# Layer 1's modulations: weighted and added by ScalarE and GpSimd during layer 0's second FFN matrix, with TensorE left to sum over the partitions

## The chip, the cores and the metric

The kernel runs on one core of one Trainium2 chip. The metric is the device time of one execution in microseconds. The core's engines work beside each other, each through its own queue in order: TensorE (PE) multiplies matrices out of SBUF into PSUM, VectorE (DVE), ScalarE (ACT) and GpSimd (POOL) work on tiles, and SyncE (SP) issues most of the DMA transfers. An engine waits for another by semaphores that the framework sets.

## The reference

The model is a trunk of two layers on 256 context tokens and 1024 latent tokens of width 1024. A conditioning vector gives each layer six modulation vectors (shift, scale and gate for the mixer and for the FFN), once for latent and once for context tokens. Cut to that and the places where it is used:

```python
for l in range(DEPTH):
    m_lat = (silu(c) @ w_mod[l] + b_mod[l])        # w_mod[l] is 1024 x 6144
    m_ctx = (silu(c_ctx) @ w_mod[l] + b_mod[l])
    sh1, sc1, ga1, sh2, sc2, ga2 = split(m_lat, 6)  # likewise for the context
    pl = modulate(rms_norm(x, g_mix[l]), sh1, sc1) @ w_in[l]
    ...                                             # four mixers, w_out, gated residual ga1
    x = x + ga2 * (squared_relu(modulate(rms_norm(x, g_ffn[l]), sh2, sc2) @ w_ffn1[l]) @ w_ffn2[l])
```

All data is float32.

## The kernel before

Activations lie with features on the partitions and tokens on the free axis: 256 context columns and two groups of 512 latent columns. Each large product is made of three matmuls on split operands (`mm3`, L141 to L143: high by high, high by low, low by high). The splits are made by ScalarE (the high part, a copy, L130) and by GpSimd (the low part, a subtraction, L246) for weights, and by VectorE (L1420) for the hidden activations.

The modulations of a layer are made in three **banks** of 2048 columns by `mod_bank` (L306). For each of eight slices k of 128 rows of `w_mod` it loads two halves of 128x1024 (L315, on SP's queue) and issues four matmuls of 128x512 (L319). Their stationary operand is `csil`, the two conditioning vectors' slice in 32 columns, so each result fills one of four 32-partition groups of a PSUM tile `po`. After eight slices ScalarE copies `po` to SBUF, four transposes (L328) turn it, and two additions on VectorE (L333) put it, with the bias, into `mods`. `mods` (the function) does this bank by bank and adds the scale vectors `ms` for banks 0 and 2.

Layer 1's three banks are made at three places. Bank 0 is made in layer 0's `ffn`, in the loop over pairs of hidden chunks (L1428): two slices after each of the first four pairs, with the halves in `u` tiles (25 buffers). Bank 1 is a stream of its own in `weave` in layer 1's first stage (L1490), beside the last part of the norm (`pending`) and the first attention projection (`p_attn`); its halves are in `e` tiles (3 buffers). Bank 2 is a third stream beside the second LRU mixer and an attention projection (L1498).

One iteration of the FFN2 loop has two chunks fc. It loads and splits two row blocks of `w_ffn2` (`wrows`: one in `wh`/`wl` tiles, one in `u` tiles), loads two chunks of activations (`e<-m`), has ScalarE copy them to `u` tiles and VectorE subtract (`act`, L1419 and L1420), and then runs 24 accumulations: eight output blocks for each of the three token groups, each of six matmuls into one of seven PSUM buffers (`pm`, `qk`, `pt`), with an evacuation by VectorE (L136) that multiplies by the gate and adds to x.

`weave` and the loops set the order in which the program is written; a list scheduler of the framework then fixes each engine's own order from it before the kernel runs.

Of the kernel before, what the change touches and what calls it, by code (L numbers as in the profile page):

```python
# [10 lines left out]
ALU = mybir.AluOpType  # L11
AX = mybir.AxisListType

P = 128
# [4 lines left out]
KD = D // P  # L19
NT = T // P  # L20
DEPTH = 2
# [7 lines left out]
C_GMIX, C_GFFN, C_BMOD, C_SCW, C_SCB, C_SD, C_SG = 0, 8, 16, 64, 88, 94, 96  # L29
# [64 lines left out]
class Net:  # L94
# [55 lines left out]
    def setup(self):  # L150
        nc = self.nc

        rnd = self.const([P, 4 * P], "rnd", F32R)
        raw = self.B(4 * P)
        nc.sync.dma_start(raw, self.I["cst"][:, 0:4 * P])
        self.copy_a(rnd, raw)
        self.identr, self.wmask = rnd[:, 0:P], rnd[:, P:4 * P]
        self.ident = f(self.identr)
        cst = self.const([P, 2 * P], "cst")
        nc.sync.dma_start(cst, self.I["cst"][:, K_LE:K_LE + 2 * P])  # L160
        self.one = self.const([P, 1], "one")
        nc.vector.memset(self.one, 1.0)
        self.le = cst[:, 0:P]
        self.ge = cst[:, P:2 * P]
        self.mhalf = self.const([P, 1], "mhalf")
        nc.vector.memset(self.mhalf, -0.5)
        cT = self.const([P, KD, 2], "cT")
        nc.sync.dma_start(cT, self.I["cT"])
        th = self.const([P, KD, 2], "cth")
        self.act(th, cT, AF.Tanh, scale=0.5)  # L170
        ch = self.const([P, KD, 2], "cth2")
        nc.vector.tensor_scalar(ch, cT, 0.5, None, op0=ALU.mult)

        self.csil = self.const([P, 2 * KD + 30], "csil")
        nc.vector.memset(self.csil, 0.0)
        self.stt(self.csil[:, 0:2 * KD].rearrange("p (k j) -> p k j", j=2), th, 1.0, ch, ALU.add, ALU.mult)
        self.L = [self.layer_params(l) for l in range(DEPTH)]

    def late_setup(self):
# [126 lines left out]
    def mod_bank(self, l, b, land, tag="po"):  # L306

        nc = self.nc
        ps = self.PS(tag)
        for k in range(KD):  # L310
            raws = []
            for hf in range(2):
                raw = f(land())[:, :1024]
# [4 lines left out]
            for cg in range(4):  # L318
# [2 lines left out]
                                 start=k == 0, stop=k == KD - 1, skip_group_check=True,  # L321
                                 tile_position=(0, 32 * cg))
            yield 1.8
        sb = self.B()
        self.copy_a(sb, ps)
        pt = self.PS(tag)
# [6 lines left out]
            nc.vector.tensor_add(m[:, 16 * b:16 * b + 16, st].rearrange("p (c q) -> p c q", c=4), v[:, :, :, st], bm)  # L333

    def mods(self, l, banks, land, tag="po"):
        nc = self.nc
        p = self.L[l]
        if "mods" not in p:
            p["mods"] = self.const([P, 48, 2], f"mods{l}")
            p["s"] = [self.const([P, 8, 2], f"ms{l}{i}") for i in range(2)]  # L340
        for b in banks:
            yield from self.mod_bank(l, b, land, tag)
            if b != 1:
                i, j, cg = (0, 1, C_GMIX) if b == 0 else (1, 4, C_GFFN)
                for st in range(2):
                    self.stt(p["s"][i][:, :, st], p["mods"][:, 8 * j:8 * j + 8, st], 1.0, p["pp"][:, cg:cg + 8],
                             ALU.add, ALU.mult)


    def load_x(self, ts):  # L350
# [1051 lines left out]
    def ffn(self, l, h, t, x_out, groups, pending, tail):  # L1402
# [17 lines left out]
                self.nc.vector.tensor_sub(al[:, t], raw[:, t], f(ah[:, t]))  # L1420
            return lambda t0, n: (ah[:, t0:t0 + n], al[:, t0:t0 + n])

        def f2(fs):
            ws = [self.wrows(w2, fc * P, self.U if fc % 2 else None) for fc in fs]
            aa = [act(fc) for fc in fs]
            return [self.acc_rows(l, 5, ws, aa, x, [g], tags) for g in groups]
        mg = self.mods(l + 1, [0], self.U) if l + 1 < DEPTH else iter(())
        for fc in range(0, NF - 2, 2):  # L1428
            for g in f2([fc, fc + 1]):
                drain(g)  # L1430
            next(mg, None)
            next(mg, None)
        drain(mg)
        tail(f2([NF - 2, NF - 1]))

    def layer(self, l, h, pending):

# [3 lines left out]
        self.queue_weights(l)  # L1441
        xd = self.xd
        md, un = {}, {}
        fill = [self.mods(l, [b], self.E) for b in (1, 2)]

        def p_attn(kind, kv, with_dt=False):
            rr = R_GC if kind == "C" else R_GD
# [220 lines left out]
```

## Time and profile before

| | |
|---|---|
| median of 3 runs | 3124.76 us (3121.27 to 3127.82) |
| profiled execution | 3125.24 us, span 3123.5 us |
| mean granted clock | 0.986 |
| TensorE, VectorE, ScalarE, GpSimd busy | 96%, 71%, 49%, 26% |

The span runs from the first to the last instruction of the profiled execution. A timeline row gives the start and the duration in microseconds, the engine, the line, the operation, the tiles written and read, the shape and the number of records; a bracket behind it tells how long the engine was idle before and which engine's work ended that. A float32 matmul leaves two records. TensorE's granted clock of 1.00 is its upper level, 2.4 GHz.

### The profile page before, as it was taken

How to read it: one execution, taken by the hardware profiler on the slowest of the kernel's cores; microseconds unless marked ns; L12 is line 12 of the kernel's file. 1: busy time of each engine (PE TensorE's matmuls, PEld its weight loads, DVE VectorE, ACT ScalarE, POOL GpSimd, SP SyncE). 2: the span in 40 equal slices, each digit the busy share in tenths (PEclk: the TensorE clock that was granted, in tenths of full speed). 3: DMA queues.
4: the chain of work that ended last, by engine and by line, in shares of the span. 5: the costliest groups of instructions: out<-in, count | busy, mean ns of one | idle time of the engine just before them, and what ended most of it. 6: DMA issues, size and time to landing. Idle time of an engine off the chain costs nothing.

```text
span 3123.5 us, 45937 instructions
## 1 busy us (share of the span) xinstructions
PE 2992.9 (96%) x16354; PEld 2477.7 (79%) x16354; DVE 2203.9 (71%) x4417; ACT 1527.6 (49%) x3602; POOL 797.9 (26%) x708
## 2 busy tenths in 40 slices
PE   6999998899999999999999999999899999999999
PEld 4688887688889887788888688787778788878887
DVE  5788777787742665577777777778887876567775
ACT  5576776675454444221112576676675544431211
POOL 2214123241454100222111512223343510032220
PEclk8999999999999999999999999999999999999999
DMA  8300012330355545642222400112322554552321
GB/s 312 99 18 25 19 37 60 108 137 29 124 159 166 172 149 176 219 154 80 77 88 78 146 23 13 28 40 80 129 82 85 172 189 150 166 183 85 105 85 58
DMA packets 241941, 335.97 MB, mean 108 GB/s; under 512 B 37424, under 2 KB 159408, under 8 KB 241712
## 3 DMA queue, kind: packets, MB, share of 16 engines
q1 hardware_dynamic: 214064, 286.88, 28.8%
q10 hardware_dynamic: 27648, 46.15, 4.1%
q8 instruction: 129, 2.11, 0.3%
q14 instruction: 100, 0.82, 0.1%
HBM read 253.28 MB, written 79.69 MB: 107 GB/s over the span
## 4 chain that ended last, share of the span: by engine, by line
PE 61%; DVE 5%; ACT 4%; DMA 2%; issue 2%; POOL 2%; ACTq 0%; SPq 0%; POOLq 0%; DVEq 0%
PE qk L143 8%; PE qk L142 8%; PE qk L141 8%; PE pm L143 7%; PE pm L141 6%; PE pm L142 6%; PE pt L142 3%; PE pt L143 3%; PE pt L141 3%; DVE u L136 1%; PE pt L747 1%; PE po L756 1%; PE po L757 1%; POOL wl L246 1%; ACT s L130 1%
## 5 line engine op out<-in xcount | busy, mean ns | idle before, releaser
L246 POOL TENSOR_TENSOR wl<-raw,wh 128x512 fp32r<-128x512 f32 (+1 forms) x224 | 317.7, 1432 | 1229.5 <-ACT wh L130 1130.3
L141 PE MATMUL pm<-u,wh 128*128 128x512 f32 (+1 forms) x1270 | 474.0, 374 | 4.4 <-DVE u L136 2.8
L143 PE MATMUL pm<-u,wl 128*128 128x512 f32 (+1 forms) x1270 | 466.8, 368 | 1.3 <-POOL wl L246 1.3
L142 PE MATMUL pm<-u,wh 128*128 128x512 f32 (+1 forms) x1270 | 465.8, 367 | 0.0
L130 ACT ACTIVATE wh<-raw 128x512 fp32r<-128x512 f32 (+1 forms) x224 | 135.7, 628 | 476.6 <-PE qk L142 165.4
L143 PE MATMUL qk<-u,wl 128*128 128x512 f32 (+1 forms) x876 | 328.0, 375 | 1.8 <-POOL wl L246 1.8
L141 PE MATMUL qk<-u,wh 128*128 128x512 f32 (+1 forms) x876 | 325.6, 373 | 1.6 <-ACT wh L130 1.5
L130 ACT ACTIVATE s<-pt 128x512 fp32r<-128x512 f32 (+4 forms) x548 | 251.2, 467 | 122.1 <-PE pt L747 76.2
L142 PE MATMUL qk<-u,wh 128*128 128x512 f32 (+1 forms) x812 | 301.4, 371 | 1.9 <-POOL u L438 1.5
L136 DVE SCALAR_TENSOR_TENSOR u<-pm,mods,u 128x512 f32<-128x512 f32 (+1 forms) x312 | 215.5, 692 | 91.1 <-PE pm L143 90.0
L141 PEld LDWEIGHTS pm<-u,wh 128*128 128x128 f32 x1270 | 243.4, 192 | 41.3 <-DVE u L136 4.3
L143 PEld LDWEIGHTS pm<-u,wl 128*128 128x128 f32 x1270 | 242.5, 191 | 35.1 <-POOL wl L246 2.7
L142 PEld LDWEIGHTS pm<-u,wh 128*128 128x128 f32 x1270 | 243.2, 192 | 30.6
L136 DVE SCALAR_TENSOR_TENSOR u<-qk,mods,u 128x512 f32<-128x512 f32 (+1 forms) x296 | 204.8, 692 | 84.5 <-PE qk L143 83.6
L133 ACT ACTIVATE b<-b 128x512 f32<-128x512 f32 (+4 forms) x256 | 146.1, 571 | 151.8 <-DVE b L1372 120.2
L133 ACT ACTIVATE e<-qk,t 128x512 f32<-128x512 f32 (+2 forms) x336 | 188.3, 571 | 42.8 <-DVE t L680 27.3
L751 DVE TENSOR_TENSOR s<-pt,s 128x512 fp32r<-128x512 f32 (+1 forms) x256 | 166.5, 659 | 40.9 <-ACT s L130 36.7
L1420 DVE TENSOR_TENSOR u<-e,u 128x256 fp32r<-128x256 f32 (+1 forms) x160 | 160.7, 1021 | 47.0 <-ACT u L130 23.7
L141 PEld LDWEIGHTS qk<-u,wh 128*128 128x128 f32 x876 | 166.0, 190 | 33.9 <-ACT wh L130 2.0
L143 PEld LDWEIGHTS qk<-u,wl 128*128 128x128 f32 x876 | 165.4, 189 | 32.7 <-POOL wl L246 2.6
L142 PEld LDWEIGHTS qk<-u,wh 128*128 128x128 f32 x812 | 153.4, 189 | 31.1 <-POOL u L438 2.2
L141 PE MATMUL pm<-wh,u 128*128 128x256 f32 (+1 forms) x592 | 175.7, 298 | 2.0 <-ACT b L133 1.7
(341 smaller groups left out, 7582.3 us busy)
## 6 DMA issues: line engine op xcount, KB each, us to landing
raw<-in_w_ffn SPq DMA_DIRECT2D x184, 256.0 KB, 3.0
e<-in_w_mod SPq DMA_DIRECT2D x64, 512.0 KB, 4.5
u<-in_w_ffn SPq DMA_DIRECT2D x60, 512.0 KB, 5.1
m<-b ACTq DMA_DIRECT2D x96, 256.0 KB, 2.0
e<-m SPq DMA_DIRECT2D x32, 640.0 KB, 4.2
u<-in_w_mod SPq DMA_DIRECT2D x32, 512.0 KB, 6.8
e<-m SPq DMA_DIRECT2D x32, 512.0 KB, 4.0
xd<-u SPq DMA_DIRECT2D x24, 640.0 KB, 3.2
```

The lines of the kernel that those rows point to most:

```text
L130: return self.nc.scalar.activation(o, i, AF.Copy, **k)
L133: self.nc.scalar.activation(o, i, fn, **k)
L136: self.nc.vector.scalar_tensor_tensor(o, a, s, b, op0=op0, op1=op1)
L141: mm(o, ah, bh, start=start, stop=False, skip_group_check=part)
L142: mm(o, ah, bl, start=False, stop=False, skip_group_check=part)
L143: mm(o, al, bh, start=False, stop=stop, skip_group_check=part)
L246: self.nc.gpsimd.tensor_sub(l, raw, f(h))
L747: nc.tensor.transpose(pt[:, e * 256 + hd * P:e * 256 + hd * P + P], prs[hd][0][:, (i + e) * P:(i + e) * P + P], self.ident)
L751: nc.vector.tensor_sub(tl, pt[:, :w], f(th))
L756: nc.tensor.matmul(po[:, :256], V[:, kc, :], th[:, c], start=i + e == 0, stop=False)
L757: nc.tensor.matmul(po[:, :256], V[:, kc, :], tl[:, c], start=False, stop=i + e == len(kcs) - 1)
L1420: self.nc.vector.tensor_sub(al[:, t], raw[:, t], f(ah[:, t]))
```

## The change

Layer 1's banks are all made in layer 0's FFN2 loop by a new generator, `mods_side`, and no longer by `mod_bank`; layer 0's own banks are as before. For each bank and each half of 1024 columns there are two running sums `acc`, one for each conditioning vector, in `u` tiles. Each of eight steps loads one half slice of `w_mod`. At the first step ScalarE copies it twice with the conditioning vector's slice as a per-partition scale, straight into the sums (128x1024). At each later step ScalarE makes four scaled copies of 128x512 in `s` tiles (8 buffers) and GpSimd adds them to the sums: 168 copies and 168 adds in all. After eight steps four matmuls with `pick1` (a column of ones, moved by one for the second vector) sum over the partitions, two accumulating into each 32-partition group: first both vectors of one group, then both of the next. There are six such reductions, 24 matmuls in place of 96. `mod_post` is the old end of `mod_bank`, three times in this loop. Four steps follow the first pair of chunks, three each later pair, and two the last before the tail. Besides, both layers' loops now load and split the next pair's weights ahead of the current pair's matmuls, and layer 1's two fill streams are empty.

```diff
+        self.pick1 = self.const([P, 34], "pick1")
+        nc.vector.memset(self.pick1, 0.0)
+        nc.vector.memset(self.pick1[:, 1:2], 1.0)
...
+    def mods_side(self, l, land):
...
+        for b in range(3):
+            ps = self.PS("po")
+            for hf in range(2):
+                acc = [land()[:, :1024] for _ in range(2)]
+                for k in range(KD):
+                    raw = land()[:, :1024]
+                    c0 = 2048 * b + 1024 * hf
+                    nc.sync.dma_start(raw, self.I["w_mod"][l, k * P:(k + 1) * P, c0:c0 + 1024])
+                    for st in range(2):
+                        cond = self.csil[:, 2 * k + st:2 * k + st + 1]
+                        if k == 0:
+                            self.copy_a(acc[st], raw, scale=cond)
+                            continue
+                        for q in range(2):
+                            c, t = slice(512 * q, 512 * q + 512), self.S()
+                            self.copy_a(t, raw[:, c], scale=cond)
+                            nc.gpsimd.tensor_add(acc[st][:, c], acc[st][:, c], t)
+                    yield
+                for q in range(2):
+                    cg = 2 * hf + q
+                    for st in range(2):
+                        nc.tensor.matmul(ps[32 * cg:32 * cg + 32, :], self.pick1[:, 1 - st:33 - st],
+                                         acc[st][:, 512 * q:512 * q + 512], start=st == 0, stop=st == 1,
+                                         skip_group_check=True, tile_position=(0, 32 * cg))
+            self.mod_post(l, b, ps, "po")
+            self.mods_scale(l, b)
...
-        mg = self.mods(l + 1, [0], self.U) if l + 1 < DEPTH else iter(())
+        mg = self.mods_side(l + 1, self.U) if l + 1 < DEPTH else iter(())
+        ws = ws2([0, 1])
         for fc in range(0, NF - 2, 2):
-            for g in f2([fc, fc + 1]):
+            gs = f2([fc, fc + 1], ws)
+
+            ws = ws2([fc + 2, fc + 3])
+            for g in gs:
                 drain(g)
-            next(mg, None)
-            next(mg, None)
+            for _ in range(3 if fc else 4):
+                next(mg, None)
         drain(mg)
...
-        fill = [self.mods(l, [b], self.E) for b in (1, 2)]
+        fill = [self.mods(l, [b], self.E) if l == 0 else iter(()) for b in (1, 2)]
```

How the instructions stand now is shown at three places; lines of the changed kernel are its own (L328 is L336 there, L429 is L475). First ScalarE in one iteration of the FFN2 loop, where `u<-e` are the copies of the next pair's activations and `wh<-raw` and `u<-raw` those of weights. Before:

```order
L130 ACTIVATE wh<-raw 128x512 x2
L130 ACTIVATE u<-raw 128x512 x2
L130 ACTIVATE u<-e 128x256
L130 ACTIVATE u<-e 128x512 x2
L130 ACTIVATE u<-e 128x256
L130 ACTIVATE u<-e 128x512 x2
```

After, in the iteration behind the end of a bank (`b<-po` is the copy of the finished bank, `s<-u,csil` are the scaled copies):

```order
L130 ACTIVATE u<-raw 128x512 x2
L130 ACTIVATE b<-po 128x512
L130 ACTIVATE u<-e 128x256
L130 ACTIVATE s<-u,csil 128x512 x12
L130 ACTIVATE u<-e 128x512 x2
L130 ACTIVATE u<-e 128x256
L130 ACTIVATE u<-e 128x512 x2
L130 ACTIVATE wh<-raw 128x512 x2
```

Twelve scaled copies now stand between the first 256-column copy of the next pair and all of its 512-column copies; GpSimd's adds stand in the same order, behind its two splits of the `u` weights. Next TensorE between two iterations of that loop, before:

```order
L142 MATMUL pm<-u 128x512
L143 MATMUL pm<-u 128x512
L319 MATMUL po<-u,csil 32x512 x8
L141 MATMUL qk<-u,wh 128x256
L142 MATMUL qk<-u,wh 128x256
L143 MATMUL qk<-u,wl 128x256
```

And after, with the four matmuls of a reduction (`pick` is the column of ones) and the transposes of the finished bank:

```order
L143 MATMUL pt<-u 128x512
L389 MATMUL po<-u,pick_94 32x512 x4
L141 MATMUL qk<-u,wh 128x256
L142 MATMUL qk<-u,wh 128x256
L143 MATMUL qk<-u,wl 128x256
L141 MATMUL qk<-u 128x256
L142 MATMUL qk<-u 128x256
L143 MATMUL qk<-u 128x256
L336 MATMUL po<-rnd,b 128x128 x4
L141 MATMUL pm<-u,wh 128x256
```

Eight matmuls on `csil` after each of four iterations have gone; four on `pick` stand after six iterations, and after three of these the transposes follow six matmuls later. Last, TensorE in layer 1's first stage ahead of the transposes that spread the norm of the last latent group (L429 before, L475 after). Before:

```order
L141 MATMUL pm<-wh,u 128x264
L142 MATMUL pm<-wl,u 128x264
L143 MATMUL pm<-wh,u 128x264
L319 MATMUL po<-e,csil 32x512 x4
L429 MATMUL pt<-rnd,t 128x128 x4
L141 MATMUL pm<-wh,u 128x264
```

After:

```order
L141 MATMUL pm<-wh,u 128x264
L142 MATMUL pm<-wl,u 128x264
L143 MATMUL pm<-wh,u 128x264
L475 MATMUL pt<-rnd,t 128x128 x4
L141 MATMUL pm<-wh,u 128x264
L142 MATMUL pm<-wl,u 128x264
```

The four matmuls ahead of the norm's transposes have gone, and the order around them is the same.

## Rows read from the trace of the kernel before

**Rows 1.** the page's shares: busy us, share of the span, instructions of each engine

```profile
PE 2992.9 (96%) x16354; PEld 2477.7 (79%) x16354; DVE 2203.9 (71%) x4417; ACT 1527.6 (49%) x3602; POOL 797.9 (26%) x708
```

**Rows 2.** busy time by stretch: its limits, length, engines, granted clock, DMA share, GB/s

```profile
1298.00:1328.00 30.00, 30.00 (x164) 24.07 (x160) 19.95 (x31) 5.04 (x11) 5.63 (x4) 1.00 0.45 149
1475.00:1503.00 28.00, 28.00 (x147) 23.73 (x146) 20.29 (x31) 5.12 (x10) 5.49 (x5) 1.00 0.25 85
1720.00:1781.00 61.00, 56.35 (x362) 40.13 (x361) 47.04 (x102) 32.63 (x74) 32.62 (x26) 1.00 0.48 161
2150.00:2235.00 85.00, 72.16 (x450) 54.88 (x449) 74.89 (x135) 56.10 (x99) 31.62 (x21) 0.96 0.42 126
```

**Rows 3.** timeline of TensorE: start, duration, line, tiles, records, [idle before]

```profile
1297.62 1.92 PE L319 MATMUL po<-u,csil 128*32 128x512 f32 x16
1299.48 0.39 PE L141 MATMUL pt<-u,wh 128*128 128x256 f32 x1
...
1753.58 1.06 PE L319 MATMUL po<-e,csil 128*32 128x512 f32 x8
1754.57 0.65 PE L429 MATMUL pt<-rnd,t 128*128 128x128 f32 x4
...
1758.07 1.81 PE L319 MATMUL po<-e,csil 128*32 128x512 f32 x8
1759.81 0.44 PE L638 MATMUL qk<-rnd,b 128*128 128x128 f32 x2
```

**Rows 4.** groups of 1300 to 1650 us by form: count, busy us, mean ns, idle before

```profile
L246 POOL TENSOR_TENSOR wl<-raw,wh 128x512 fp32r<-128x512 f32 x26 | 38.0, 1479 | 192.5 <-ACT wh L130 192.3
L130 ACT ACTIVATE u<-e 128x512 fp32r<-128x512 f32 x54 | 30.7, 616 | 0.0
L1420 DVE TENSOR_TENSOR u<-e,u 128x512 fp32r<-128x512 f32 x53 | 54.3, 1031 | 2.3 <-ACT u L130 2.3
```

**Rows 5.** timeline of GpSimd and VectorE, two places

```profile
1445.69 2.87 POOL L246 TENSOR_TENSOR wl<-raw,wh 128x512 fp32r<-128x512 f32 x2 [20.06 <-ACT wh L130]
1447.67 1.44 DVE L1420 TENSOR_TENSOR u<-e,u 128x512 fp32r<-128x512 f32 x1
1454.90 0.68 DVE L1420 TENSOR_TENSOR u<-e,u 128x512 fp32r<-128x512 f32 x1
...
1741.18 4.68 POOL L407 TENSOR_TENSOR s<-s 128x512 f32<-128x512 f32 x3 [0.42 <-ACT s L133]
1741.59 3.12 DVE L407 TENSOR_TENSOR s<-s 128x512 f32<-128x512 f32 x2 [0.28 <-ACT s L133]
```

**Rows 6.** layer 1's first stage: chain by line, its pieces, and timeline rows

```profile
by line: PE po L319 14.2%; PE pm L143 11.4%; PE pm L141 11.4%; PE pm L142 10.2%; DMA e<-in_w_mod 6.4%; POOL s L407 6.0%; issue 4.4%; ACT s L133 4.3%; POOL u L438 3.9%; POOL t L599 3.5%; PE pt L413 2.4%; DVE b L603 2.2%; DVE b L610 1.7%; POO
1779.22 0.44 PE po L328 x4
1780.99 0.14 PE pm L143
1724.16 0.28 PE L141 MATMUL pm<-wh,u 128*128 128x264 f32 x1
1746.07 0.68 DVE L409 TENSOR_TENSOR s<-s 128x512 f32<-128x512 f32 x1
1749.67 0.95 PE L413 MATMUL pt<-one,s 128*128 128x1 f32 x8
1767.73 0.38 ACT L130 ACTIVATE u<-qk 128x256 fp32r<-128x256 f32 x1 [2.23 <-PE qk L638]
1769.70 1.45 POOL L438 TENSOR_TENSOR u<-s,u 128x512 fp32r<-128x512 f32 x1
```

**Rows 7.** third bank's stage: pieces of the chain, and TensorE's waits (us, times, longest)

```profile
2192.12 0.99 PE po L319 x8
2223.77 0.45 PE po L328 x4
PE po L319 <- DMA e<-in_w_mod: 1.4, 1, 1.4
```

More of the change, by code (lines that the diff above doesn't have):

```diff
@@ L323, in mod_bank, with mod_post @@
             yield 1.8
+        self.mod_post(l, b, ps, tag)
+    def mod_post(self, l, b, ps, tag):
+        nc = self.nc
         sb = self.B()
@@ L335, in mods, with mods_tiles @@
     def mods(self, l, banks, land, tag="po"):
-        nc = self.nc
+        self.mods_tiles(l)
+        for b in banks:
+            yield from self.mod_bank(l, b, land, tag)
+            self.mods_scale(l, b)
+    def mods_tiles(self, l):
         p = self.L[l]
@@ L340, in mods, with mods_scale @@
             p["s"] = [self.const([P, 8, 2], f"ms{l}{i}") for i in range(2)]
[L341 to L347, printed above, removed]
+    def mods_scale(self, l, b):
+        p = self.L[l]
+        if b != 1:
+            i, j, cg = (0, 1, C_GMIX) if b == 0 else (1, 4, C_GFFN)
+            for st in range(2):
+                self.stt(p["s"][i][:, :, st], p["mods"][:, 8 * j:8 * j + 8, st], 1.0, p["pp"][:, cg:cg + 8],
+                         ALU.add, ALU.mult)
+    def mods_side(self, l, land):
+        nc = self.nc
+        self.mods_tiles(l)
+        for b in range(3):
[18 more added lines that the diff above has]
+                    cg = 2 * hf + q
+                    for st in range(2):
+                        nc.tensor.matmul(ps[32 * cg:32 * cg + 32, :], self.pick1[:, 1 - st:33 - st],
+                                         acc[st][:, 512 * q:512 * q + 512], start=st == 0, stop=st == 1,
+                                         skip_group_check=True, tile_position=(0, 32 * cg))
+            self.mod_post(l, b, ps, "po")
+            self.mods_scale(l, b)
     def load_x(self, ts):
@@ L1421, in act, with ws2, f2 @@
             return lambda t0, n: (ah[:, t0:t0 + n], al[:, t0:t0 + n])
-        def f2(fs):
-            ws = [self.wrows(w2, fc * P, self.U if fc % 2 else None) for fc in fs]
+        def ws2(fs):
+            return [self.wrows(w2, fc * P, self.U if fc % 2 else None) for fc in fs]
+        def f2(fs, ws):
             aa = [act(fc) for fc in fs]
             return [self.acc_rows(l, 5, ws, aa, x, [g], tags) for g in groups]
-        mg = self.mods(l + 1, [0], self.U) if l + 1 < DEPTH else iter(())
+        mg = self.mods_side(l + 1, self.U) if l + 1 < DEPTH else iter(())
+        ws = ws2([0, 1])
         for fc in range(0, NF - 2, 2):
-            for g in f2([fc, fc + 1]):
+            gs = f2([fc, fc + 1], ws)
+            ws = ws2([fc + 2, fc + 3])
+            for g in gs:
                 drain(g)
-            next(mg, None)
-            next(mg, None)
+            for _ in range(3 if fc else 4):
+                next(mg, None)
         drain(mg)
-        tail(f2([NF - 2, NF - 1]))
+        tail(f2([NF - 2, NF - 1], ws))
     def layer(self, l, h, pending):
```

## The prediction

> **What bounds the kernel now.** I read the share of busy time on the page first: TensorE is busy for 96% of the span, GpSimd for 26%, ScalarE for 49%, VectorE for 71% [rows 1]. An average over the span says little about one stage, so I went on to the busy time by stretch [rows 2]. The change touches three stretches. In layer 0's second FFN matrix, which ends at 1724.16 us [rows 6], TensorE is busy for all of both stretches shown, at a granted clock of 1.00 (2.4 GHz): an iteration takes 28 us, one that also holds modulation matmuls 30 us. There each TensorE microsecond added or removed is a microsecond of the span, as long as the others keep up. GpSimd works 5.5 us of the 28, ScalarE 5.1, VectorE 20.3; so ScalarE and GpSimd have room, VectorE has 7.7 us. In layer 1's first stage (1720 to 1781) TensorE is busy for 56 of 61 us, and the chain of waits there gives 14.2% of 75 us to the modulation matmuls and 6.4% to their loads [rows 6]: 10.7 and 4.8 us. In the stage of the third bank (2150 to 2235) TensorE is busy for only 72 of 85 us at a clock of 0.96, and VectorE for 75 [rows 2]: others bound it.
>
> **The change, part by part.** I make the sum against the profiled execution's 3125.24 us and then move it to the median.
>
> *Bank 0 leaves the FFN2 loop's TensorE.* A batch of two k steps (8 matmuls, 16 records) occupies TensorE from 1297.62 to 1299.48 [rows 3], 1.86 us. Four batches: -7.4 us, all on the path.
>
> *Six reductions come in.* Each has four matmuls of 128x512, two per 32-column group one after the other. The trace has no such piece; it has these of the same shape. Four matmuls on four different groups take 0.99 us (1753.58 to 1754.57), so different groups run together. Two rounds on the same four groups take 1.86 us, so a second round on a group adds 0.87. Two pairs, one behind the other, take 1.74 us (1758.07 to 1759.81) [rows 3]. In the order group 0, group 0, group 1, group 1 the second matmul must wait for the first and the third stands behind it; the third can run beside the second, the fourth follows: three rounds, 0.99 + 2 x 0.87 = 2.7 us. Six give +16.4 us. If group 1 could pass the waiting matmul it would be two rounds, 1.74 and +10.4 us; if nothing overlapped, four rounds, 0.99 + 3 x 0.87 = 3.6 and +21.6. I take three, since the queue's order stands between the end values. The Trainium skill ("TensorE: Matmul & The Clock Gate", Part 3: Packing small matmuls) has matmuls start and end strictly in the order of the program; by that it is three rounds, +16.4. No run here shows this order yet.
>
> *Closing each bank.* The four transposes (0.44 us [rows 6]) now stand three times in this loop, before once: +0.9. Ahead of them ScalarE copies the bank out of PSUM in about 0.62 us (the duration of this shape [rows 4]), while TensorE has six matmuls of 256 columns as cover. An iteration has 48 matmuls of 256 and 96 of 512 columns, so a matmul of 256 has 28/240 = 0.12 us and one of 512 0.23; six of the first are 0.7 us. With the hand-over on both sides about 0.2 us are bare each time: +0.6 (0 to 2).
>
> *ScalarE and GpSimd beside TensorE.* An iteration gets three steps: 12 copies on ScalarE and 12 adds on GpSimd (where a half begins, 8 and two copies of 1024). A copy of 128x512 costs 0.62 us, so ScalarE has 5.1 + 12 x 0.62 = 12.5 of 28 us. GpSimd's splits of this shape cost 1.48 us [rows 4], and three adds beside VectorE's adds took 4.68 [rows 5], 1.56 each: 4 splits and 12 adds are 16 x 1.48 = 23.7 us, 25 at 1.56. It fits, tightly. What can reach TensorE is order. ScalarE's 12 copies stand ahead of the next pair's 512-column copies, and a scratch pool of 8 buffers lets it run only 8 ahead of GpSimd. GpSimd first has two weight splits (about 3 us), then must finish four adds (6 us): the twelfth copy runs about 10 us into the iteration, and the next pair's copies right behind it. VectorE has placed the subtractions that wait for them behind 8 evacuations of 256 and 3 of 512 columns, which by TensorE's pace is 8 x 6 x 0.12 + 3 x 6 x 0.23 = 10 us into the iteration. So VectorE waits for little, and seven PSUM accumulators give TensorE 7 x 6 x 0.23 = 9.7 us of cover. If that cover were gone, each late microsecond would be one of the span. The subtractions get slower: 0.68 us alone, 1.44 where GpSimd works [rows 5], a mean of 1.03 now [rows 4]. Four of them and two small ones add at most 3 us to VectorE's 20.3 of 28. The last half before the tail is the tightest: 20 adds in one iteration are 28 to 31 us, and its reduction waits for the last of them, 0 to 5 us, with all of TensorE's queue behind it. ScalarE's copy of a finished bank waits for a reduction in turn, and behind it stand the next pair's copies; it comes at the head of an iteration, where these have time. A step's load needs one of 25 tiles, of which eight hold x, twelve two pairs and two the sums; three are left, so it waits for a release, but a step has 9 us. In sum +2 (0 to 15). The weights of the next pair, loaded one iteration earlier, are what keeps GpSimd's splits out of this; in layer 1's loop, where TensorE is busy throughout and GpSimd idle, that is worth nothing. SP's queue holds the same number of loads; three per iteration instead of four in four iterations, at a DMA share of 0.25 against 0.45 [rows 2], cost nothing.
>
> FFN2 together: -7.4 + 16.4 + 0.9 + 0.6 + 2 = **+12.5** (+4 to +32).
>
> *Layer 1's first stage loses bank 1.* At most the chain's 15.5 us come back, and 0.4 for the transposes. But the norm of the last latent group goes on beside it. Its sum is ready at 1746.75, and TensorE reads it only at 1749.67 [rows 6]: 2.9 us late, which vanish, and then TensorE waits there instead. Between there and the transposes at 1754.57 stands one batch of 0.99: together -3.9. The norm's eight steps follow, to 1771.15, with ScalarE held once for 2.2 us by a TensorE result that stood behind batches (1767.73) [rows 6]; I take half of it, -1.1. Then to the stage's end TensorE has two more batches and the transposes, -2.4. That is **-7.4** (-3 to -16).
>
> *The third bank's stage* has 0.99 and 0.45 of it on the chain, and 1.4 us of TensorE waiting for a load [rows 7]: **-2** (0 to -8, the bank's 8 batches of 0.99). No queue that is left has to wait longer: SP only loses loads in both stages.
>
> Sum: 12.5 - 7.4 - 2 = +3.1. The profiled execution is 0.5 us above the median of 3124.76; so the forecast is 3124.8 + 3.1 = **3127.9**.
>
> **The rivals.**
> *A, faster.* The reductions take two rounds (10.4), nothing stalls, and layer 1 gives back its chain share: 10.4 - 7.4 + 1.5 - 15.5 - 3 = -14, 3111 us. For it: TensorE is busy 92% of the first stage. Against: TensorE's wait for the norm, just worked out.
> *B, slower.* VectorE and GpSimd hold each other up. A subtraction that meets GpSimd's operations ends only when these do (1447.67 took 1.44 beside 1445.69's two) [rows 5]. If a whole string of 12 adds goes first, 12 x 1.48 = 17.8 us, TensorE runs dry after 9.7 us. It decides from the point where the next pair's subtractions end later than some 20 us into an iteration. Five iterations have the string ahead of all 512-column copies: 5 x 8 = 40 us at worst, half of it likely: 12.5 + 20 - 9.4 = +23, 3148 us. Against: VectorE's two adds took 1.56 each beside GpSimd's three of 1.56, so they take turns [rows 5]. The Trainium skill ("SBUF — State Buffer", Who interferes with whom) says that a VectorE operation with two SBUF inputs and a GpSimd one that reads SBUF exclude each other for a whole instruction; the trace agrees (0.68 against 1.44), and the time by it is B's if GpSimd wins each turn, the forecast's if they alternate.
> *C, no gain in layer 1.* The matmuls leave but the norm and VectorE hide it: 12.5 - 3 = +9.5, 3134 us. For it: VectorE is busy 75 of 85 us in the third bank's stage.
>
> **How the numbers follow.** Chances: forecast 0.42 (its own range 3120 to 3135), A 0.27, B 0.16, C 0.15. About 0.2%, 6.2 us, is what a measurement of this kernel can tell from no change. Of the forecast's 0.42 some 0.28 lie within it, 0.11 above and 0.03 below; A gives 0.25 faster and 0.02 within; B is slower; C is 0.11 slower and 0.04 within. Faster 0.28, same 0.34, slower 0.38. The range of 8 in 10 leaves a tenth on each side: 3109 (most of A) to 3147 (half of B).
>
> **What would show it.** In the profile after: the time from each reduction's first matmul to the next other matmul (2.7, or 1.7, or 3.6); TensorE's idle time in FFN2 and who ended it (VectorE's evacuations or GpSimd's adds would be B); the interval between GpSimd's weight splits, 28 us where nothing stalls; the mean of VectorE's 512-column subtraction (1.0 to 1.4); in layer 1, the time from the end of FFN2's loop on TensorE to the first stage's end (57 us before, from 1724.16 to 1780.99 [rows 6]; 49 by the forecast, 41 by A, 54 and more by C), and there a TensorE wait for the norm's sum. I am wrong if FFN2 grows by under 4 or over 32 us, or if layer 1's two stages give more than 16 us.

## The result and the profile after

The changed kernel takes 3171.76 us (median of four runs, 3166.67 to 3176.22) against 3123.38 us: a ratio of 1.0153 [1.0133, 1.0172], some 48 us slower (here and below, a ratio with its 95% interval is estimated from all runs of both kernels and is not the quotient of the medians). The forecast was 3127.9 us with a range of 3109 to 3147. The profiled execution took 3171.14 us, its span is 3169.4 us and its mean granted clock 0.972 (0.986 before).

The page's shares of the changed kernel, which answer to [rows 1]:

```profile
PE 2990.5 (94%) x16210; PEld 2495.0 (79%) x16210; DVE 2233.3 (70%) x4419; ACT 1647.1 (52%) x3782; POOL 1024.6 (32%) x876
```

TensorE is busy as long as before, in a span 45.9 us longer. The place shows in one row: layer 1's first stage begins on TensorE at 1724.16 us before [rows 6], and now at

```profile
1770.43 0.28 PE L141 MATMUL pm<-wh,u 128*128 128x264 f32 x1
```

46.3 us later, although the kernel was 2.4 us ahead at 877 us, where the norm ahead of layer 0's FFN is read. At the end of the span the difference is 45.9: the whole loss, 48.7 us, arises in layer 0's FFN, and layer 1 gives nothing back. (The FFN2 loop is the last part of that stretch; over the whole of it `e_prefetch` and `e_nofill` below differ from before by 0.2 us at most.) TensorE's waits from 1260 to 1800 us in the kernel after (us in total, times, longest):

```profile
PE qk L141 <- DVE u L136: 17.5, 3, 8.4
PE pm L141 <- DVE u L136: 9.2, 2, 8.7
PE pt L141 <- DVE u L136: 5.9, 1, 5.9
PE pm L141 <- ACT dtr L130: 4.8, 1, 4.8
```

The first three lines are FFN2: TensorE finds no free PSUM buffer, since VectorE's evacuations are late. Five of these waits (8.71, 4.84, 5.89, 4.33 and 8.35 us) are 32.1 of 32.6 us; before, the longest wait in FFN2 is 0.6 us. The first of them, in the kernel after, on four engines and SP's queue (a row of SP's is the issue of a load):

```profile
1308.25 3.47 DVE L1466 TENSOR_TENSOR u<-e,u 128x512 fp32r<-128x512 f32 x2 [3.90 <-ACT u L130]
...
1301.89 17.07 POOL L384 TENSOR_TENSOR u<-u,s 128x512 f32<-128x512 f32 x12
1318.91 2.57 POOL L250 TENSOR_TENSOR wl<-raw,wh 128x512 fp32r<-128x512 f32 x2
...
1320.23 1.61 SPq L262 DMA_DIRECT2D raw<-in_w_ffn  x2
...
1322.37 0.42 SPq L375 DMA_DIRECT2D u<-in_w_mod  x1
...
1322.84 0.63 ACT L130 ACTIVATE u<-raw 128x512 fp32r<-128x512 f32 x1 [11.71 <-DMA raw<-in_w_ffn]
...
1327.94 2.56 ACT L130 ACTIVATE s<-u,csil 128x512 f32<-128x512 f32 x4 [2.73 <-DMA u<-in_w_mod]
1330.40 0.61 ACT L130 ACTIVATE wh<-raw 128x512 fp32r<-128x512 f32 x1
1334.14 2.19 ACT L130 ACTIVATE u<-u,csil 128x1024 f32<-128x1024 f32 x2 [3.12 <-DMA u<-in_w_mod]
1336.23 2.79 ACT L130 ACTIVATE u<-e 128x256 fp32r<-128x256 f32 x6
...
1336.67 0.43 DVE L1466 TENSOR_TENSOR u<-e,u 128x256 fp32r<-128x256 f32 x1 [12.74 <-ACT u L130]
...
1337.54 0.79 PE L141 MATMUL pm<-u,wh 128*128 128x512 f32 x1 [8.71 <-DVE u L136]
```

Read it from the end. TensorE waits for an evacuation that stands on VectorE behind a subtraction; the subtraction waits for ScalarE's copy `u<-e`, which is ready to run, but stands in ScalarE's queue behind scaled copies and weight copies. These wait for loads, and the loads stand in SP's queue one behind the other: the `w_mod` load of 1322.37 behind the `raw` load of 1320.23, which needs one of two `raw` buffers. A buffer comes free when GpSimd has split its weights (1318.91), and this split stands behind twelve adds. The next slice's load, at 1330.52, was issued just as ScalarE's copies of this slice ended (1327.94 and 2.56 us), so that one also had to wait for a `u` tile. So one of GpSimd's strings holds up, through one release, three queues.

After each wait TensorE also ran at its lower level. Two windows (limits, length, busy time of each engine, clock, DMA share, GB/s):

```profile
1335.00:1340.00 5.00, 2.46 (x6) 1.98 (x7) 3.33 (x8) 4.48 (x9) 0.00 (x0) 0.50 0.51 161
1345.00:1350.00 5.00, 5.00 (x24) 4.11 (x23) 5.00 (x8) 0.00 (x0) 2.74 (x2) 1.00 0.26 61
```

The granted clock is 0.50, 1.2 GHz, behind the wait and 1.00 ten us later. In five such stretches of 3.9 to 5.7 us, 57 matmuls of 512 columns took 24.7 us from start to start, 0.43 each in place of 0.23: 11.5 us more. (A row's duration overlaps the next matmul's start; at the upper level it reads 0.40.) The fifth wait looks different, in the last iteration before the tail:

```profile
1704.53 24.99 POOL L384 TENSOR_TENSOR u<-u,s 128x512 f32<-128x512 f32 x20 [2.37 <-ACT s L130]
1729.46 2.58 POOL L250 TENSOR_TENSOR wl<-raw,wh 128x528 fp32r<-128x528 f32 x2
...
1720.79 11.52 DVE L1466 TENSOR_TENSOR u<-e,u 128x256 fp32r<-128x256 f32 x1 [4.93 <-ACT u L130]
...
1734.76 0.41 DVE L1466 TENSOR_TENSOR u<-e,u 128x256 fp32r<-128x256 f32 x1
...
1733.03 0.80 PE L141 MATMUL qk<-u,wh 128*128 128x512 f32 x1 [8.35 <-DVE u L136]
```

Here the copy was there at 1720.79. One subtraction of 256 columns, 0.41 us when alone, took 11.52: it ended 0.3 us after GpSimd's string, of which nine operations followed each other beside it without a gap, 1.22 to 1.26 us from start to start. In the string of 1301.89 the two sides took turns instead: GpSimd's adds took 1.42 each, VectorE's subtractions of 1308.25 1.74 each.

The reductions and transposes:

```profile
1360.12 1.92 PE L389 MATMUL po<-u,pick 128*32 128x512 f32 x8
1361.97 0.39 PE L141 MATMUL qk<-u,wh 128*128 128x256 f32 x1
...
1456.11 0.65 PE L336 MATMUL po<-rnd,b 128*128 128x128 f32 x4
1456.52 0.36 PE L141 MATMUL pm<-u,wh 128*128 128x256 f32 x1
```

A reduction occupies TensorE for 1.85 us, the transposes for 0.41. So FFN2's account is: reductions 6 x 1.85 - 7.4 = +3.7, transposes +0.8, waits +32.6, lower clock +11.5, together 48.6 of the 48.7 us measured (46.3 + 2.4). That it closes to a tenth is partly luck, since records overlap.

Layer 1's first stage now lasts from 1770.43 to 1824.45, 54.0 us instead of 56.7 (1724.16 to 1780.8). The two stages' windows, answering to [rows 2], and the longest wait:

```profile
1771.00:1828.00 57.00, 45.77 (x304) 43.33 (x305) 47.45 (x102) 33.83 (x81) 32.22 (x26) 0.85 0.12 38
2200.00:2285.00 85.00, 61.28 (x382) 55.20 (x381) 74.19 (x140) 53.23 (x100) 31.06 (x24) 0.83 0.17 47
...
1786.83 0.59 PE L141 MATMUL pm<-wh,u 128*128 128x264 f32 x1 [4.85 <-ACT dtr L130]
```

TensorE has a bank's eight batches (0.99 us each [rows 7]) less to do in each, and its granted clock fell from 1.00 to 0.85 and from 0.96 to 0.83. It runs ahead, waits for ScalarE, and continues with matmuls of 0.22 us from start to start in place of 0.12. The 2.7 us that the first stage gains are gone at the norm ahead of layer 1's FFN (2420 us before): there the kernel is 48.6 us behind.

### The profile page after: what moved, and what is told of

Read it like the earlier page. It is cut to its first block, busy times and chain, and to the rows that moved or that the text cites. A ratio compares the mean times of both kernels' runs of the same rounds, so it can differ in the third digit from the quotient of the medians.

```text
span 3169.4 us, 46172 instructions
## 1 busy us (share of the span) xinstructions
PE 2990.5 (94%) x16210; PEld 2495.0 (79%) x16210; DVE 2233.3 (70%) x4419; ACT 1647.1 (52%) x3782; POOL 1024.6 (32%) x876
## 5 line engine op out<-in xcount | busy, mean ns | idle before, releaser
L141 PE MATMUL qk<-u,wh 128*128 128x512 f32 (+1 forms) x876 | 327.1, 374 | 20.4 <-DVE u L136 17.5
L384 POOL TENSOR_TENSOR u<-u,s 128x512 f32<-128x512 f32 x168 | 235.0, 1436 | 39.1 <-ACT s L130 39.0
L1466 DVE TENSOR_TENSOR u<-e,u 128x256 fp32r<-128x256 f32 (+1 forms) x160 | 182.8, 1156 | 86.7 <-ACT u L130 71.8
L141 PEld LDWEIGHTS qk<-u,wh 128*128 128x128 f32 x876 | 166.1, 190 | 53.5 <-DVE u L136 18.6
```

The lines of the kernel that those rows point to most:

```text
L141: mm(o, ah, bh, start=start, stop=False, skip_group_check=part)
L384: nc.gpsimd.tensor_add(acc[st][:, c], acc[st][:, c], t)
```

## The experiments

The theory after the result was: GpSimd's strings delay the weight splits, and through the `raw` buffers the loads (**queues**). The rivals: a subtraction is held by a whole string (**hold**); the loads or ScalarE's copies alone; the removed matmuls of layer 1 or the earlier weights. The expectations use letters: Q is the queues, P (port) is that VectorE and GpSimd hold each other up, L the loads alone; R (ring) is the round of one slice, a load into the one free `u` tile, four scaled copies, the next load; W (warm) is that layer 1's stages lose their gain because TensorE's clock falls there.

**Which of the added work stalls FFN2.** Three kernels take work out of the changed one. `e_noadds` drops all of GpSimd's adds, `e_loads` the copies as well, `e_oneadd` half of the adds:

```diff
# e_noadds
-                            nc.gpsimd.tensor_add(acc[st][:, c], acc[st][:, c], t)
# e_loads: the copies to t as well
# e_oneadd
+                            if st == 0:
                                 nc.gpsimd.tensor_add(acc[st][:, c], acc[st][:, c], t)
```

> Leaves out GpSimd's 168 adds (the scaled copies stay, their results are not summed). Theory Q (queues): the strings of adds hold GpSimd's weight splits back, these hold the two raw buffers, SP's queue holds the modulations' loads behind the weight loads that wait for those buffers, ScalarE waits in order for the modulations' loads with the next pair's copies behind it, and VectorE and TensorE follow. Then without adds TensorE's idle time in the FFN2 loop falls from 32.6 us to under 6 and no half-clock stretch follows: about 3130 us. Rival L (loads): three 512-KB loads per iteration into three spare tiles are too slow by themselves, whoever sums: idle time stays over 20 us, 3150 us or more. Rival P (port): VectorE and GpSimd hold each other up in SBUF: as Q, about 3130.

> Leaves out ScalarE's copies and GpSimd's adds of steps two to eight, and keeps all 48 loads, the six reductions and the transposes. Q and P: no idle time in the FFN2 loop; it costs 6 x 1.85 - 7.4 + 0.8 = 4.5 us more than before: 3126 to 3130 us. L: idle time of 10 us or more stays.

> The changed kernel with the adds of one conditioning vector left out (84 of 168; the other vector's copies are made but not summed). R: the ring gets 8 us shorter and fits into 28: idle time under 10 us, 3128 to 3140 us. If idle time goes with the number of adds that meet subtractions (port): about half of it stays, 16 us and its half-clock stretches, 3146 to 3152.

Measured: 3126.24 and 3128.57 us (one run each, before 3122.72), and 3124.21 us, 1.0005 [0.9995, 1.0014]. None has a stall in FFN2. TensorE's longest waits from 1260 to 1800 us in `e_noadds` all lie in layer 1:

```profile
PE pm L141 <- ACT dtr L130: 4.8, 1, 4.8
PE pm L143 <- POOL u L483: 4.5, 4, 1.8
```

From 877 us to layer 1 their profiled executions are 3.3, 2.2 and 1.9 us longer than before's. So the loads, the copies, the reductions and the earlier weights together cost less than the 3.7 + 0.8 of the account; the stalls need GpSimd's adds, and more than half of them.

**Are long strings needed?** `e_spread` puts one step after each token group, in place of three after each pair (the first pair keeps its fourth):

```diff
                 drain(g)
-            for _ in range(3 if fc else 4):
+                next(mg, None)
+            if not fc:
                 next(mg, None)
```

> One step after each token group of a pair in place of three after the pair; copies, adds, loads and reductions are all kept. Q: strings of four adds instead of twelve let the weight splits and the loads pass in between; TensorE's idle time in the loop falls from 32.6 to under 12 us, 3135 to 3145 us. P: as many adds meet as many subtractions, idle time stays near 33 us and the time near 3172. L: as P.

Measured: 3169.68 us, 1.0150 [1.0135, 1.0165], waits of 7.48, 5.43, 5.58, 3.71 and 1.98 us. The expectation failed: the scheduler strings the adds together all the same, as GpSimd's and VectorE's rows of `e_spread` show at the first wait, which here is a hold:

```profile
1303.35 14.98 POOL L384 TENSOR_TENSOR u<-u,s 128x512 f32<-128x512 f32 x12
1318.28 2.49 POOL L250 TENSOR_TENSOR wl<-raw,wh 128x512 fp32r<-128x512 f32 x2
...
1309.72 12.20 DVE L1466 TENSOR_TENSOR u<-e,u 128x512 fp32r<-128x512 f32 x2 [3.54 <-ACT u L130]
```

Twelve adds run at 1.25 us, as if alone, and the first of two subtractions ends with them and the two splits behind. Where the steps are written does not set which adds stand together.

**The queues themselves.** `e_raw3` gives the changed kernel a third `raw` buffer, at the price of one `b` tile; `e_braw3` does the same to the kernel before:

```diff
-        ... tag="b", name="b", bufs=5)[:, :n]
+        ... tag="b", name="b", bufs=4)[:, :n]
-        ... tag="raw", name="raw", bufs=2)[:, :n]
+        ... tag="raw", name="raw", bufs=3)[:, :n]
```

> The changed kernel with three raw buffers for weights in place of two, paid for with one b tile (four in place of five). If the first four stalls come from weight loads on SP's queue that wait for a raw buffer behind GpSimd's adds, with the modulations' loads behind them, ScalarE's waits for those loads get shorter and the idle time of these four (23.8 us) falls by half or more: 3150 to 3160 us. If starvation behind strings of adds is what counts, it moves elsewhere or grows, as with the b tiles: 3165 or more, with subtractions of over 8 us.

> Before with three raw buffers instead of two and four b tiles instead of five; nothing else. It splits what e_raw3 measured (3141.8): there the stages ahead of layer 0's second FFN matrix were 10.3 us earlier than before's by 877 us, and the FFN2 loop 21 us longer. Theory: the earlier stages gain from the third buffer on their own, so this kernel is 8 to 11 us faster than before by 877 us, unchanged in the FFN2 loop (no stalls there before), and 3111 to 3120 in all. Rival: the 10 us were scatter or belong to the other edit, 3121 to 3126.

Measured: `e_raw3` 3141.79 us, 1.0057 [1.0042, 1.0072]; `e_braw3` 3118.11 us, 0.9991 [0.9982, 1.0001]. The first four waits fell from 23.8 us to 7.2 (2.42, 1.48, 2.04, 1.29). ScalarE's wait for weights, from 1260 us to the loop's end, first in the kernel after and then in `e_raw3`:

```profile
ACT u L130 <- DMA raw<-in_w_ffn: 110.8, 19, 11.7
```

```profile
ACT u L130 <- DMA raw<-in_w_ffn: 32.4, 5, 7.0
```

In the kernel before it is 31.7 us up to 1720 us.

The fifth stayed, 7.22 us, and its rows in `e_raw3` are the hold again:

```profile
1669.81 24.94 POOL L384 TENSOR_TENSOR u<-u,s 128x512 f32<-128x512 f32 x20 [1.28 <-ACT s L130]
1694.72 1.29 POOL L250 TENSOR_TENSOR wl<-raw,wh 128x528 fp32r<-128x528 f32 x1
...
1686.04 10.25 DVE L1466 TENSOR_TENSOR u<-e,u 128x256 fp32r<-128x256 f32 x1 [5.08 <-ACT u L130]
```

The third buffer also gains 10 us ahead of FFN2, in both kernels alike (-10.3 and -10.0 us by 877 us). So `e_raw3`'s FFN2 loop is 21.1 us longer than before's (from -10.3 to +10.8), while the after kernel's is 48.7; against `e_braw3`, whose loop is 3.1 shorter (-10.0 to -13.1), it is 24.2 longer. The missing buffer accounts for about half of the loss, and for most of the first four waits. In `e_braw3` part of the gain is lost in layer 1 (-13.1 at 1725 us, -6.3 at 2420), and the total is about unchanged.

**Other buffers for the slices.** `e_btiles` loads the slices into `b` tiles, `e_fix` does that with four `raw` buffers:

```diff
-                    raw = land()[:, :1024]
...
+                    raws = [self.B() for _ in range(2)]
...
# e_fix besides: raw bufs=4, up bufs=24
```

> The changed kernel with the modulations' slices loaded as two 128x512 halves into the five small b tiles, which this loop leaves free, in place of one u tile; all copies, adds and reductions stay. Theory R (ring): with three steps per iteration the ring 'load into the one u tile that is free, four scaled copies, load again', the adds, the weight split behind them and the next weight load takes longer than an iteration's 28 us, and without the adds a little less. If the shortage of u tiles is the half of it that matters, loads now run ahead: TensorE's idle time in the loop falls from 32.6 to under 12 us, 3130 to 3145 us. If the adds ahead of the weight splits decide alone (raw buffers, SP's queue): it stays over 25 us, 3160 or more.

> As the run with b tiles, and four raw buffers for weights in place of two (paid for with one u tile, 24 in place of 25), so that the next weight loads don't wait for GpSimd's splits behind the adds. R: both halves of the ring are cut, idle time under 6 us: 3126 to 3132 us, the cost of the reductions and the lost gain of layer 1 alone. If VectorE and GpSimd holding each other up is the cause, the idle time stays near 30 us.

Measured: 3213.86 us, 1.0280 [1.0260, 1.0299], and 3240.22 us, 1.0372 [1.0357, 1.0388]: both far slower, against what the queues alone would give. Neither frees the queues cleanly, since five `b` tiles are a short store for the slices: ScalarE waits 38.5 us for them in `e_btiles` and 50.6 in `e_fix`. In `e_btiles` the longest wait of TensorE, 13.5 us, ends behind 16.9 us in which VectorE waited for ScalarE, whose copies stood behind scaled copies that waited for slices; its longest subtraction, 11.5 us, lies elsewhere. In `e_fix` the wait for weights fell to 18.1 us, and GpSimd's strings get longer; VectorE's four subtractions and one string there:

```profile
1359.88 24.90 POOL L385 TENSOR_TENSOR u<-u,s 128x512 f32<-128x512 f32 x20
1384.72 2.50 POOL L250 TENSOR_TENSOR u<-raw,u 128x512 fp32r<-128x512 f32 x2
1387.16 2.50 POOL L250 TENSOR_TENSOR wl<-raw,wh 128x512 fp32r<-128x512 f32 x2
1389.60 2.68 POOL L250 TENSOR_TENSOR u<-raw,u 128x512 fp32r<-128x512 f32 x2
...
1377.03 16.74 DVE L1467 TENSOR_TENSOR u<-e,u 128x256 fp32r<-128x256 f32 x4 [3.51 <-ACT u L130]
```

The first of the four subtractions took 14.1 us of these 16.74 and ended beside the string's last two operations; another, at 1301.21, took 17.5. TensorE waited up to 27.4 us at a time, and a hold stands in each of its four longest waits (27.4, 15.5, 14.5 and 12.0 us). So these two runs don't tell what free queues alone would give; they show how much a hold can cost.

**Is a string enough for a hold?** `e_string` gives the kernel before twelve adds on scratch tiles per iteration, with no more loads:

```diff
+                self.copy_a(sb, f(aa[0](256, 512)[0]))
+                for _ in range(12):
+                    self.nc.gpsimd.tensor_add(sa, sa, sb)
```

> The kernel before with twelve adds on GpSimd per iteration of layer 0's FFN2 loop between two scratch tiles (one filled by a ScalarE copy of that iteration's activations, so that they stay in it); their result is unused, there are no more loads and no scaled copies. It measures the adds by themselves. Starvation: a subtraction of VectorE with both inputs in SBUF waits for a whole string of adds without gaps, so single ones take over 8 us (0.68 alone), TensorE idles and its clock falls: 20 us or more above 3123. If VectorE and GpSimd take turns, no subtraction takes over 1.8 us and the time stays within 5 us of 3123.

Measured: 3143.94 us, 1.0068 [1.0051, 1.0085], with waits of 5.14 and 9.48 us, but no subtraction took over 1.79 us. There was no hold, and the run says only that a string by itself need not make one. The waits have another source. The longer one, on GpSimd, ScalarE and TensorE:

```profile
1417.33 17.13 POOL L1429 TENSOR_TENSOR s<-s 128x512 f32<-128x512 f32 x12
1434.42 2.48 POOL L246 TENSOR_TENSOR wl<-raw,wh 128x512 fp32r<-128x512 f32 x2
...
1438.50 0.63 ACT L130 ACTIVATE u<-raw 128x512 fp32r<-128x512 f32 x1 [16.80 <-DMA raw<-in_w_ffn]
1439.03 0.40 ACT L130 ACTIVATE u<-e 128x256 fp32r<-128x256 f32 x1
...
1441.20 0.80 PE L141 MATMUL pm<-u,wh 128*128 128x512 f32 x1 [9.48 <-DVE u L136]
```

ScalarE waits for a load of weights, with the copies of activations behind it in its queue. The load waits for a `raw` buffer, and GpSimd frees that only when it has done twelve adds and the splits behind them. (ScalarE's scratch copy waited for adds too, up to 11.3 us, but that ended at 1416.14, well ahead of this.) Ahead of the wait of 5.14 us ScalarE waited 7.89 and 3.04 us for such loads. So this run shows the queues by themselves: the adds and two `raw` buffers are enough, without scaled copies and without a load that the kernel before doesn't have. What decides between turns and a hold stays open.

**Fewer banks.** `e_bank0` makes only bank 0 the new way (one step per pair), `e_bank01` banks 0 and 1 (two steps); the others stay in layer 1:

```diff
-        for b in range(3):
+        for b in banks:          # (0,) or (0, 1)
...
-            for _ in range(3 if fc else 4):
+            for _ in range(1 if fc else 2):   # e_bank01: 2 if fc else 4
```

> Only bank 0 goes the new way, one step of copies and adds per pair of chunks (two after the first); layer 1's banks 1 and 2 stay where they were. Q: strings of four adds stall nothing; two reductions of 1.85 us take the place of four batches of 1.86: -3.7 us, 3118 to 3121 us. P: 4 adds per iteration give a third of the idle time, some 10 us more and half-clock stretches: 3130 or more.

> Banks 0 and 1 the new way, two steps per pair of chunks; bank 2 stays in layer 1. R: two steps' ring takes some 20 us and fits: idle time under 5 us; four reductions 7.4 for four batches 7.4, one more set of transposes 0.4, nothing from layer 1's first stage: 3122 to 3128 us. Port: two thirds of the idle time, 20 us, and half-clock stretches, 3150 or more.

Measured: 3127.07 us, 1.0011 [0.9999, 1.0024], and 3129.49 us, 1.0020 [1.0010, 1.0029]. With 4, 8 and 12 adds per pair the loss is 3, 6 and 48 us; from 877 us to layer 1, in the profiled executions, it is 0.5, 13.1 and 48.7. So it grows far faster than the work (`e_bank01` has waits of 6.61 and 1.89 us). The gain of 3.7 us expected of bank 0 did not come in that stretch: one wait of 2.22 us and the slower matmuls behind it (1.7 us) took it. That execution lost 7.5 us more in layer 1, where only the earlier weights differ, and `e_bank0`'s runs scatter widely (3118.78 to 3136.24).

**What layer 1 gives back.** `e_nofill` is the kernel before without banks 1 and 2 of layer 1. `e_warm` is the changed kernel with 64 matmuls on constants where the two fill streams stood. `e_prefetch` is the kernel before with only the earlier weights:

```diff
# e_nofill
+        fill = [self.mods(l, [b], self.E) if l == 0 else iter(()) for b in (1, 2)]
# e_warm
+        fill = [self.mods(l, [b], self.E) if l == 0 else self.warm() for b in (1, 2)]
# e_prefetch
+            ws = ws2([fc + 2, fc + 3])
```

> The kernel before without layer 1's banks 1 and 2 (loads, matmuls and transposes left out, the values set to zero). It prices what layer 1 can give back at all. The prediction's step: -9.4 us, 3114 us. Theory W (warm): without these matmuls TensorE idles in both stages, its granted clock falls to half there as after the change (0.85 and 0.83), and the gain is lost: within 3 us of 3123.4.

> The changed kernel with 64 matmuls on a constant tile put where layer 1's banks 1 and 2 stood, their results unused, no loads and no transposes. W: the granted clock in the first stage and in the third bank's stage rises from 0.85 and 0.83 to 0.95 or more, and TensorE's 16 us or more of added work cost nothing: 3172 us or up to 4 less. Without W, the added matmuls delay the norm as they did before: 5 to 10 us more, 3177 to 3182.

> The kernel before with the next pair's weights loaded and split one iteration ahead, nothing else. Prediction: nothing, 3123.4 within 2 us. Rival: two more u tiles in use and GpSimd's splits at another time make loads late: 5 us or more slower.

Measured: `e_nofill` 3124.99 us, 1.0006 [0.9996, 1.0015]; `e_warm` 3172.55 us, 1.0152 [1.0139, 1.0166]; `e_prefetch` 3123.29 us, 0.9994 [0.9985, 1.0003]. The earlier weights are worth nothing, and neither is the removal of 64 matmuls of 512 columns, 32 in each of two stages. In `e_nofill`, from 1724 and from 2150 us:

```profile
1724.00:1781.00 57.00, 44.43 (x312) 41.63 (x311) 47.49 (x100) 33.78 (x81) 33.12 (x26) 0.94 0.15 48
2150.00:2235.00 85.00, 64.46 (x390) 58.19 (x389) 74.31 (x125) 54.70 (x95) 28.48 (x21) 0.88 0.13 37
...
1741.97 0.59 PE L141 MATMUL pm<-wh,u 128*128 128x264 f32 x1 [4.85 <-ACT dtr L130]
1749.40 0.95 PE L413 MATMUL pt<-one,s 128*128 128x1 f32 x8
```

TensorE waits there, and reads the norm's sum at 1749.40. Its first stage began at 1725.51, 1.35 us later than before's, so this is 23.9 us into the stage; before it was 25.5, and in the kernel after 24.6. The sum is ready 22.6 us into the stage in all three: the 2.9 us by which TensorE read it late became 1.3 in `e_nofill` and 2.0 in the kernel after, since matmuls of the projection still stand ahead of it. `e_warm`'s two windows:

```profile
1771.00:1828.00 57.00, 53.02 (x376) 41.97 (x376) 47.75 (x100) 35.91 (x85) 33.81 (x28) 1.00 0.14 43
2200.00:2285.00 85.00, 71.15 (x473) 57.54 (x472) 72.72 (x146) 53.30 (x102) 31.47 (x24) 0.94 0.17 47
```

The useless work brings the clock back to 1.00 and 0.94 and costs nothing: the whole run is as long as after's. So the two stages can carry that many matmuls free. In the profiled executions the stretch from layer 1's start to the norm at 2420 us takes 696.2 us before, 698.6 after, 699.3 in `e_nofill` and 694.7 in `e_warm`. So the matmuls on constants seem even to win some 4 us there, but the time of the whole run does not show it: what follows, unchanged code, took 10 us longer in that execution of `e_warm` than in the kernel after's.

**A version that beats both.** `e_moved` leaves the old matmuls as they are and makes layer 1's bank 0 in layer 0's stage of the first LRU mixer, where VectorE bounds; `e_mraw3` adds the third `raw` buffer:

```diff
-        mg = self.mods(l + 1, [0], self.U) if l + 1 < DEPTH else iter(())
+        mg = iter(())
+        ahead = self.mods(l + 1, [0], self.E) if l + 1 < DEPTH else iter(())
-        weave((m_lru(0), DL[9]), (p_lru(1), 26))
+        weave((m_lru(0), DL[9]), (p_lru(1), 26), (ahead, 15))
```

> The kernel before with layer 1's bank 0 made by the old matmuls, but in layer 0's stage of the first LRU mixer and the second LRU projection instead of the FFN2 loop. If that stage is bound by VectorE like the third bank's stage, the 7.4 us of the loop come back: 3115 to 3118 us. If TensorE bounds it: 3123 or more.

> The kernel e_moved (layer 1's bank 0 made in layer 0's last LRU stage, 3115.6) with three raw buffers and four b tiles. If the two gains are apart from each other, 8.7 and about 8 to 10: 3104 to 3109. If the third buffer gains nothing by itself: 3113 to 3118.

Measured: `e_moved` 3115.62 us, 0.9968 [0.9956, 0.9980]; `e_mraw3` 3113.78 us, 0.9973 [0.9961, 0.9985]. Thirty us of that stage, first in the kernel before and then in `e_moved`:

```profile
580.00:610.00 30.00, 21.44 (x162) 18.05 (x161) 27.08 (x66) 10.37 (x24) 12.75 (x11) 0.93 0.31 107
```

```profile
580.00:610.00 30.00, 25.02 (x187) 20.20 (x185) 26.76 (x62) 12.92 (x27) 13.33 (x11) 1.00 0.37 124
```

VectorE is the busy engine, TensorE has room, and with more to do its clock rises to 1.00. By 877 us `e_moved` is where before is (-0.5), and when FFN2 is over it is 11 us ahead. FFN2 is then free of modulations, and TensorE is busy for all of 1300 to 1400 us.

The third buffer adds nothing that these runs can tell, although 3104 to 3109 was expected if the two gains add up.

## Why the prediction was wrong

By its own steps:

- *Bank 0 out, -7.4.* Right as far as the runs tell: `e_moved`, which takes the bank out of the loop and puts it into another stage, is 8.7 us faster by the medians (6 to 14 us by the interval), and its stretch from 877 us to layer 1 is 10.5 us shorter.
- *Six reductions, +16.4.* Mis-sized: 6 x 1.85 = 11.1, two rounds, the lower bound (1.74) rather than three. Their records start in pairs 14 ns apart (1360.123 and .137, 1360.578 and .591), so two ran beside each other throughout; which matmul of which group is in a pair, the records don't tell. The third round, which I took from the queue's order, did not come. The Trainium skill ("TensorE: Matmul & The Clock Gate", Part 3: Packing small matmuls) has matmuls start and end strictly in program order; by that it would be three rounds, 2.7, if the queue held them in the order in which they are written, and the measured 1.85 is two. Whether the queue's order is another, or TensorE doesn't keep it, no run here shows.
- *Transposes +0.9, closing +0.6.* 0.41 each, +0.8; and no idle time in front of them.
- *ScalarE and GpSimd beside TensorE, +2 (0 to 15).* **This is the step that failed**: 32.6 us of waits and 11.5 of lower clock, 44.1; FFN2 grew by 48.7 us, beyond the 32 that was named as a sign of being wrong. I summed what each engine has to do in 28 us and found that it fits, tightly. It does fit: an add takes 1.44 us, a scaled copy 0.71. But the step checked order only along one path, ScalarE's copies and the scratch tiles. It let three sentences pass alone that are one chain: the splits behind the adds ("what keeps GpSimd's splits out of this"), SP's queue ("cost nothing"), and the step's load ("a step has 9 us"). GpSimd's split frees the `raw` buffer, the buffer lets SP issue, and SP's order holds the next slice. The lower clock after a wait wasn't in the sum at all; a late microsecond cost 1.35 (44.1 over 32.6), not one.
- *Rival B* named a mechanism that is there, the hold, and gave it a chance of 0.16. The argument against it, that the two engines take turns [rows 5], holds in some strings and not in others. The Trainium skill ("SBUF — State Buffer", Who interferes with whom) says that a VectorE instruction with two SBUF inputs contends with a GpSimd instruction that reads SBUF, and that the lock on the shared ports is exclusive; the trace agrees that one waits for the other (11.52 us against 0.41), but here a subtraction was out for nine of GpSimd's. In the kernel after, a hold stands only in the last wait; B's 3148 lacks the queues.
- *First stage -7.4, third bank's stage -2.* Neither came; that is rival C. The first stage is 2.7 us shorter (54.0 us, C's sign), and the gain is gone by 2420 us (+48.6). I took the chain's matmuls for time, but TensorE was the filler of a stage that others bound. With less to do its clock fell too; that the fall took the gain isn't shown, since `e_warm`, with the clock back, is no faster as a whole.

With 11.1 for the reductions, 44.1 in the failed step and nothing from layer 1 the sum is -7.4 + 11.1 + 0.8 + 44.1 = +48.6, 3173 us. That the queues make the most of the first four waits is shown by `e_raw3`, `e_string` and the kernels without adds. That a hold makes the last one isn't shown. The rows of the kernel after and of `e_raw3` have it there, but `e_warm`, whose loop is written the same, has 2.88 us in place of the 11.52. Its loop lost 46.0 us all the same: there the end of the loop waited 1.74 us for an evacuation and 4.70 for ScalarE's copy of the finished bank, which stood behind weight copies that waited for loads (12.60). So the code doesn't decide whether a hold comes, no run switches it alone, and without it the last iteration stalls too.

## What to carry to other kernels

Where an engine gets work up to 85% of an iteration (24 of 28 us here), don't ask whether it fits but which buffers it frees and which in-order queue waits for that; follow the release through the DMA queue to the next engine, and price TensorE's wait with its slow restart. Matmuls that fill a stage bound by other engines can be free, and taking them out gained nothing here; moving work into such a stage from one that TensorE bounds is what gained here.

## What was not expected of the hardware

- A VectorE subtraction with two operands in SBUF waited for eight and more GpSimd operations without a gap between them: 11.52, 10.25 and 11.6 us in three kernels, 17.5 in `e_fix`, against 0.41 to 0.68 alone and 1.74 where they take turns. In two kernels whose loop is written the same it took 11.52 and 2.88 us.
- After waits of 4 to 9 us TensorE's matmuls of 512 columns took 0.43 us from start to start instead of 0.23, for 3.9 to 5.7 us.
- Removing a bank's matmuls, some 8 us of TensorE's work, from a stage lowered its granted clock from 1.00 to 0.85, and 32 matmuls on constants raised it to 1.00 again without a change in the time of the whole run.
